# Transposes in place of float32 matmuls, and a new order around q and v, in a hybrid decoder layer

## The chip, the cores and the metric

The kernel runs on one core of a Trainium2 chip, as one launch. The metric is the device time of that launch in microseconds; the median of several runs counts. TensorE is called PE here, VectorE DVE, ScalarE ACT, GpSimd POOL and SyncE SP, as in the profile.

## The reference

One decoder layer on 1024 positions of 1024 features, in float32. A combined input projection feeds two branches, which are gated, merged and added to x; a gated MLP with a short convolution follows.

```python
def rmsnorm(x, gain):
    xf = x.astype(jnp.float32)
    y = xf * lax.rsqrt(jnp.mean(xf * xf, axis=-1, keepdims=True) + NORM_EPS)
    return (y * gain.astype(jnp.float32)).astype(x.dtype)
...
        h = rmsnorm(x, mix_norm[l])
        proj = h @ w_in[l]
        q, k, v, su, sv, g_a, g_b = jnp.split(proj, splits, axis=-1)
        y_att = sliding_window_attention(q, k, v, q_norm[l], k_norm[l], sinks[l])
        y_sgu = chunked_spatial_gating(su, sv, sgu_norm[l], w_s[l], b_s[l])
        merged = (jax.nn.sigmoid(g_a) * (y_att @ w_oa[l])
                  + jax.nn.sigmoid(g_b) * (y_sgu @ w_ob[l]))
        x = x + merged @ w_out[l]
        x = x + conv_gated_mlp(rmsnorm(x, ffn_norm[l]), w_up[l], conv_w[l], conv_b[l], w_down[l])
```

The attention has 8 query heads and 2 key heads of 64 features, a window of 128 positions, and RMS norms of q and k. The MLP is 2816 wide.

## The kernel before

Activations lie transposed, features on the 128 partitions and positions along the free axis. Nearly all products are split: a float32 operand becomes a high and a low part of a faster type (float32r), and three matmuls (high by high, high by low, low by high) stand for one. The large products of the gates, the output projection and the MLP go through a seven-product scheme on half matrices.

The order on each engine is the order in which the code is written (a manual schedule); each engine works through its queue in order and waits where a semaphore says so. So a line that moves in the code moves on its engine's queue, and everything behind it waits with it.

Four places matter.

**The prelude** (lines 427 to 473). k and v have been projected into two PSUM tiles (`pkv`, one for each half of the positions, k and v beside each other). `ss8` holds the sums of x's squares per position, filled by `tsquare`. `k_ms`, `k_norm`, `k_trans`, `k_hi`, `k_lo` and `k_twice` scale k, transpose it and write its high and low parts into `kT`. `v_evac` scales v by `rstd` and takes it out of `pkv` into `vt`. `rstd` is one vector operation and one power on POOL over all eight columns (lines 444 and 451). Between these stand the first four blocks of q: `q_proj` (PE), `q_sq`, `q_ms`, `q_norm` (the scaled block `qr`), `q_trans` (PE, tile `pqt`) and `q_split` (tile `qs`). Half-bank PSUM tiles (`PH`) rotate through four buffers: the matmuls into a tile wait until the readers of the tile four allocations earlier are done. The tiles of the scores (`sc`) take the two buffers that `pkv` had.

**The attention loop** (lines 698 to 745), 20 turns `n`. In turn `n`, PE computes the scores of block `n`, a first filler of other work, the transposes of block `n-2`'s probabilities (`p_trans`, tile `pt`), in eight of the turns from 2 to 13 a second filler (`u_chunk`, twelve 512-column matmuls into `pu`), and then `q_trans(n + 2)`. `q_split(n + 2)` on ACT and DVE follows. In turn 0 `rms_rows` makes `rstd_b`, the eight scale columns as one row over all 1024 positions, repeated on all partitions: a matmul of a repeated column by the identity, in eight pieces (tile `rb`).

**The sum of squares for the second norm** (`ssq_cols`, line 1747, called in `first_pair`, line 1829). `sq2` holds squares summed over the feature tiles; a float32 matmul by a column of ones sums over partitions, in eight pieces of 128 positions. DVE copies the eight columns out, scales them, POOL raises them to -0.5.

**The second broadcast** (`rms`, line 1886, called in `fast_pair` at line 1918) runs `rms_rows` on that result, behind the first product of the next pair. The squares' sum and this broadcast use the same PSUM tile `pb`, the two banks of the next pair's `zv`.

Of the kernel before, what the change touches and what calls it, by code (L numbers as in the profile page):

```python
# [10 lines left out]
F = mybir.dt.float32  # L11
# [3 lines left out]
ALU = mybir.AluOpType  # L15
AX = mybir.AxisListType

S = 1024
D = 1024
# [21 lines left out]
def body(ctx, tc, nc, a):  # L41
# [72 lines left out]
    sink_b = base.tile([128, 8], F, name="sink_b")  # L114
    ident = base.tile([128, 128], F, name="ident")
    rstd_b = base.tile([128, 1024], F, name="rstd_b")
    ones = base.tile([128, 2], F, name="ones")
    mh05 = base.tile([128, 8], F, name="mh05")
    rstd = base.tile([128, 8], F, name="rstd")
    nc.gpsimd.memset(rstd_b[:, 0:128], 1.0)  # L120
    nc.gpsimd.memset(ones, 1.0)
    nc.gpsimd.memset(mh05, -0.5)
    g2 = cp[:, 0:8]
    ng2 = sink_b
# [10 lines left out]
    def rms_rows(pb, col, hs=(0, 1)):  # L135

        for h, p in zip(hs, pb):
            for s in range(4):
                c = 4 * h + s
                nc.tensor.matmul(p[:, s * 128:(s + 1) * 128], col[:, c:c + 1].to_broadcast([128, 128]), ident,  # L140
                                 start=True, stop=True)
        for h, p in zip(hs, pb):
            nc.scalar.copy(rstd_b[:, h * 512:(h + 1) * 512], p)  # L143

# [93 lines left out]
    def tsquare(t):  # L238
        v = xt[t // 4][:, t % 4, :]
        if t in (5, 7):  # L240
            nc.vector.tensor_tensor_reduce(out=v, in0=v, in1=v, scale=1.0, scalar=0.0, op0=ALU.mult, op1=ALU.add,
                                           accum_out=ss8[:, t:t + 1])
            return
        nc.scalar.activation(v, v, AF.Square, accum_out=ss8[:, t:t + 1])
# [130 lines left out]
    def k_ms(h):  # L375
        ss = slice(4 * h, 4 * h + 4)
        nc.vector.tensor_scalar(eps_x[:, ss], ss8[:, ss], EPS / D, EPS * EPS, op0=ALU.mult, op1=ALU.add)
        nc.vector.scalar_tensor_tensor(krs3[:, ss], kss3[:, ss], 1.0 / 64,
                                       eps_x[:, ss].unsqueeze(2).to_broadcast([128, 4, 2]),
                                       op0=ALU.mult, op1=ALU.add)  # L380
        nc.gpsimd.tensor_tensor(krs[:, 8 * h:8 * h + 8], krs[:, 8 * h:8 * h + 8], mh05, op=ALU.pow)
# [32 lines left out]
    def v_evac(h):  # L414
        ss = slice(4 * h, 4 * h + 4)
        nc.vector.tensor_tensor(vt[:, ss, :], pk4[h][:, :, 128:256],
                                rstd[:, ss].unsqueeze(2).to_broadcast([128, 4, 128]), op=ALU.mult)

    def v_split():

        for g in range(2):
            vg_ = vt[:, :, 64 * g:64 * g + 64]
            vh_, vl_ = vhl[:, :, g, 64 * g:64 * g + 64], vhl[:, :, g, 64 - 64 * g:128 - 64 * g]
            copy_hi(vh_, vg_)
            nc.vector.tensor_tensor(vl_, vg_, vh_.bitcast(F), op=ALU.subtract)
# [2 lines left out]
    k_sq(0)  # L428
    k_sq(1)
    k_ms(0)  # L430
    tsquare(4)
    tsquare(5)
    q_proj(0)
# [3 lines left out]
    tsquare(6)  # L437
    q_proj(1)
    tsquare(7)
    q_norm(0)  # L440
    q_sq(1)
    q_ms(1)
    k_ms(1)
    nc.vector.tensor_scalar(rstd, ss8, 1.0 / D, EPS, op0=ALU.mult, op1=ALU.add)
    k_trans(0)
    k_hi(0)
    q_proj(2)
    k_lo(0, (0,))
    q_norm(1)
    k_lo(0, (1,))  # L450
    nc.gpsimd.tensor_tensor(rstd, rstd, mh05, op=ALU.pow)
    k_twice(0)
    q_trans(0)
    q_proj(3)
    q_sq(2)
    q_ms(2)
    k_norm(1)
    q_split(0)
    copy_hi(u_next[0], u_raw[0])
    nc.gpsimd.tensor_tensor(u_next[1], u_raw[0], u_next[0].bitcast(F), op=ALU.subtract)  # L460
    v_evac(0)
    q_norm(2)
    q_trans(1)
    k_trans(1)
# [233 lines left out]
    for n in range(20):  # L698
        if 4 <= n < 12:
            pv_mm(n - 4)  # L700
        if n < 16:
            s_mm(n)
            s_mask(n)
        if 0 <= n - 1 < 16:
            s_exp(n - 1)
        if n < 16:
            s_max(n)
        if 12 <= n:
            pv_mm(n - 4)
        q_new = filler(n, 0)  # L710
        if n == 0:
            for h in (0, 1):
                rms_rows([PH("rb")], rstd, (h,))
        if 0 <= n - 2 < 16:
            p_trans(n - 2)
        filler(n, 1)
        if 0 <= n - 4 < 16:
            pv_out(n - 4)
        for q in q_new:
            q_sq(q)  # L720
            q_ms(q)
        if 0 <= n - 2 < 16:
            p_split(n - 2)
        weights(n)
        if n in (0, 2, 4, 5):
            wo_copy((n + 1) // 2)
        if n in (7, 9, 11, 13):
            wo_add((n - 7) // 2)
        if n == 15:
            rows_again(0)  # L730
        if n == 17:
            x_gain(0, (0, 1))
        if n == 18:
            x_gain(0, (2, 3))
        if n == 19:
            x_sums((0, 1), True)
            x_sums((2, 3), True)
        for t, p in u_done:
            nc.vector.tensor_tensor(uT[:, t, :], p, rstd_b, op=ALU.mult)
        u_done.clear()  # L740
        if n + 2 < 16:
            q_trans(n + 2)
            q_split(n + 2)
        for q in [3] + q_new if n == 0 else q_new:
            q_norm(q)
# [368 lines left out]
    class Blocks:  # L1114
# [9 lines left out]
            if self.zv is not None:  # L1124
                self.v0, self.v1 = self.zv[:, L], self.zv[:, H]

        def prod(self, o, l, r, more=False):
            (wh, wl), y, nk = self.w[l], self.y[r], self.nk
            for k in range(nk):
                for j, (p, q) in enumerate(((wh, 0), (wh, 1), (wl, 0))):  # L1130
                    m = y[:, q, k, :] if nk == 4 else y[:, 2 * q + k, :]
                    nc.tensor.matmul(o, p[:, k, :], m, start=not more and k == 0 and j == 0,  # L1132
                                     stop=k == nk - 1 and j == 2, skip_group_check=True)
# [612 lines left out]

    def ssq_cols(p):
        for s in range(8):
            nc.tensor.matmul(p[:, 2 * s:2 * s + 2], pools["sq2"][:, s * 128:(s + 1) * 128], ones,
                             start=True, stop=True)  # L1750
        pool = pools["fp"]
        ss = pool.tile([128, 8], F, name="ss8b")
        nc.vector.tensor_copy(ss, p[:, 0:16].rearrange("p (s two) -> p s two", two=2)[:, :, 0])
        rsqrt_cols(ss, ss, 8, D)
        return ss

# [72 lines left out]
    def first_pair():  # L1829
        w, nx = lefts[0], lefts[1]  # L1830
        pools["mr_cm"].__exit__(None, None, None)
        pools["ex"] = ctx.enter_context(tc.tile_pool(name="ex", bufs=1, side="right", reuse_waits="tile"))
        z = PS("pz"), PS("pz")
        q, q2 = Pair(0, w.w, z[::-1]), Pair(1, nx.w)
        xu = pools["fp"].tile([128, 1024], F, tag="xu", name="xu")
        x7, u2 = xu[:, L], xu[:, H]
        x1 = pools["wx"].tile([128, 512], F, tag="x1f", name="x1f")

        q.prod(q.v1, "A11", "B11")
        a22_split()  # L1840
        nc.scalar.copy(x1, q.v1)
        fax_split()
        nx.load_p()
        nx.load_q()
        nx.load_s3()
        q.prod(q.g1, "S1", "T1")
        for e in (0, 1):
            right_split_hi("T2", e, ob["B"][:, 2 * e:2 * e + 2, :])
        for e in (0, 1):
            right_split_lo("T2", e, ob["B"][:, 2 * e:2 * e + 2, :])  # L1850
        nc.scalar.copy(u2, q.g1)
        lefts[2].load_ahead()
        q.prod(q.v0, "S3", "T3")
        square("21", 0)
        nx.adds()
        square("21", 1)
        nc.scalar.copy(x7, q.v0)
        for e in (0, 1):
            for i in (0, 1):
                d = 2 * e + i  # L1860
                p = ob["X"][e][:, i, :]
                stt(p, p, gain("21", d)[0], ob["B"][:, d, :], ALU.add)
        for e in (0, 1):
            right_split("T4", e, ob["X"][e])
        q.prod(q.g1, "S4", "B22", more=True)
        q.prod(q.g0, "A12", "B21")
        nc.vector.tensor_tensor(q.g0, q.g0, x1, op=ALU.add)
        sub(nc.vector, x7, x7, u2)
        q.prod(q.v1, "S2", "T2", more=True)
        nx.split_p()  # L1870
        q.prod(q.v0, "A22", "T4", more=True)
        pb = q2.zv
        ratio = ssq_cols(pb)
        nx.split_s3()
        nx.sum_s2()
        nx.sum_s4()
        lefts[2].adds()
        nx.split_q_half(0)
        nx.split_q_half(1)
        lefts[2].load_p()  # L1880
        nc.scalar.copy(u2, q.v1)
        q.u2 = u2
        sub(nc.vector, q.v1, x7, u2)
        sub(nc.vector, q.v0, q.v0, u2)

        def rms():

            rms_rows([pb[:, L], pb[:, H]], ratio)
            q.scale(q.zv)
            q.last_sum()  # L1890

        pools["ft_cm"] = tc.tile_pool(name="ft", bufs=1, reuse_waits="tile")
        return q, q2, rms
# [409 lines left out]
```

## Time and profile before

| | |
|---|---|
| median of 3 runs | 1157.84 us (1157.07 to 1158.2) |
| the profiled execution's own time | 1157.13 us |
| its span, first to last instruction | 1155.4 us |
| PE, POOL, DVE, ACT busy, 0 to 165 us (input projection, attention) | 163.6, 104.9, 119.4, 107.2 us |
| the same, 165 to 535 us (gating unit, gates, merge, output projection) | 369.8, 257.9, 254.1, 213.9 us |
| the same, 535 to 547 us (sum of squares, second broadcast) | 12.0, 9.7, 6.7, 4.8 us |
| the same, 547 to 1115 us (MLP) | 568.0, 285.8, 456.1, 253.5 us |
| the same, 1115 to 1155.4 us (last products, stores) | 37.0, 0, 20.7, 9.2 us |

A row of the timeline reads: start in us, duration in us, engine, line, operation, tile written and tiles read, sizes, count; in brackets the idle time before it and what ended it. Matmuls are pipelined: each is shown with its full duration, and the next one starts before it ends, so what a matmul costs PE is the distance between starts. PEld is the weight load ahead of a matmul. A row of a group (by line or by tile) has the count, the busy time and the mean duration in ns. A row of the view of waits has who waited for whom, the time in us in total, how often, and the longest.

### The profile page before, as it was taken

The page shows a single profiled execution, that of the slowest core. Times are in us where ns is not written, and L with a number is a line of the kernel's source. Part 1 is how long each engine was busy: PE and PEld are TensorE (multiplying, and loading weights), DVE is VectorE, ACT ScalarE, POOL GpSimd, SP SyncE. Part 2 cuts the span into 40 slices and gives each one's busy share as a digit, 9 for nine tenths or more (in the row PEclk, how much of TensorE's full clock was granted, in tenths as well). Part 3 has the DMA queues.
Part 4 walks back from the last instruction along what each step waited for, and adds up shares of the span by engine and source line. Part 5 has one row for each costly group of instructions (what it writes and reads, how often), then busy time and mean ns, then how long its engine had stood idle before and what let it go on. Part 6 is the DMA issues. An engine that isn't in the chain of part 4 may idle for free.

```text
span 1155.4 us, 15810 instructions
## 1 busy us (share of the span) xinstructions
PE 1150.4 (100%) x5789; PEld 978.1 (85%) x5789; DVE 857.0 (74%) x987; ACT 588.7 (51%) x896; POOL 658.3 (57%) x461
## 2 busy tenths in 40 slices
PE   9999999999999999999999999999999999999998
PEld 9999999888888888888888888888888888888887
DVE  7787747734436889887998978797788887766664
ACT  6665568643436546686444444444444354425231
POOL 1768674598783755798877676767676730000000
PEclk9999999999999999999999999999999999999999
DMA  9443565265747766644655554645464358966571
GB/s 367 149 147 67 137 217 201 74 209 174 202 108 240 240 213 237 191 143 120 165 166 149 152 137 137 173 129 145 131 171 134 111 201 308 353 220 197 176 229 56
DMA packets 86429, 204.37 MB, mean 177 GB/s; under 512 B 9616, under 2 KB 17296, under 8 KB 86160
## 3 DMA queue, kind: packets, MB, share of 16 engines
q1 hardware_dynamic: 77280, 174.93, 43.9%
q0 software_dynamic: 8544, 19.93, 10.4%
q10 hardware_dynamic: 528, 8.52, 2.1%
q8 instruction: 45, 0.74, 0.3%
q14 instruction: 32, 0.26, 0.1%
HBM read 162.70 MB, written 57.41 MB: 191 GB/s over the span
## 4 chain that ended last, share of the span: by engine, by line
PE 93%; POOL 3%; DMA 2%; DVE 1%; issue 1%; SPq 0%; ACT 0%; POOLq 0%
PE pz L1132 56%; PE pdx L2083 9%; PE pd L2083 8%; PE pY L1723 2%; PE pX L1723 2%; POOL wjl L1591 1%; PE pu L94 1%; PE pu L92 1%; PE pu L93 1%; PE pvs L94 1%; PE pvs L92 1%; PE pvs L93 1%; PE pv L568 1%; PE pq L92 1%; PE pq L93 1%; PE pq L94 1%
## 5 line engine op out<-in xcount | busy, mean ns | idle before, releaser
L1132 PE MATMUL pz<-T,qh 128*128 128x512 f32 x464 | 143.0, 389 | 0.0
L1132 PE MATMUL pz<-B,ph 128*128 128x512 f32 x352 | 108.6, 390 | 0.0
L1132 PEld LDWEIGHTS pz<-T,qh 128*128 128x128 f32 x464 | 87.0, 188 | 18.3 <-ACT u L949 0.3
L1084 POOL TENSOR_TENSOR pl<-lp,ph 128x1024 fp32r<-128x1024 f32 x30 | 73.3, 2443 | 37.0 <-ACT ph L88 37.0
L1132 PE MATMUL pz<-T,ql 128*128 128x512 f32 x232 | 90.3, 389 | 0.0
L1150 DVE TENSOR_TENSOR pz<-pz,rstd_b 128x1024 f32<-128x1024 f32 x60 | 73.9, 1232 | 6.1 <-ACT rstd_b L143 4.1
L1132 PEld LDWEIGHTS pz<-B,ph 128*128 128x128 f32 x352 | 65.9, 188 | 13.6
L1084 POOL TENSOR_TENSOR ql<-lq,qh 128x1024 fp32r<-128x1024 f32 (+1 forms) x31 | 76.4, 2488 | 0.0
L1132 PE MATMUL pz<-T,s3h 128*128 128x512 f32 x232 | 71.4, 389 | 0.0
L1132 PE MATMUL pz<-y,wjh 128*128 128x512 f32 x224 | 69.5, 391 | 0.1
L1132 PE MATMUL pz<-B,pl 128*128 128x512 f32 x176 | 68.6, 390 | 0.1
L88 ACT ACTIVATE qh<-lq 128x1024 fp32r<-128x1024 f32 (+1 forms) x31 | 31.5, 1020 | 69.3 <-POOL pl L1084 47.4
L1084 POOL TENSOR_TENSOR s3l<-lq,s3h 128x512 fp32r<-128x512 f32 x20 | 26.0, 1301 | 65.9 <-ACT s3h L88 65.9
L1372 POOL TENSOR_TENSOR wjl<-wj,wjh 128x512 fp32r<-128x512 f32 (+1 forms) x32 | 42.0, 1332 | 35.6 <-ACT wjh L88 29.8
L1132 PE MATMUL pz<-B,AX 128*128 128x512 f32 x252 | 60.6, 389 | 0.0
L1132 PE MATMUL pz<-T,AX 128*128 128x512 f32 x252 | 60.5, 389 | 0.0
L2083 PE MATMUL pdx<-bh,ah 128*128 128x512 f32 x152 | 59.2, 390 | 0.0
L2083 PE MATMUL pdx<-bh,al 128*128 128x512 f32 x152 | 59.1, 389 | 0.0
L2083 PE MATMUL pdx<-bl,ah 128*128 128x512 f32 x152 | 59.1, 389 | 0.0
L1144 ACT COPY u<-pz 128x512 f32<-128x512 f32 x28 | 16.4, 587 | 80.8 <-DVE pz L1143 80.8
L1771 DVE SCALAR_TENSOR_TENSOR tg<-pz,cp,tg 128x1023 f32<-128x1023 f32 (+1 forms) x44 | 56.2, 1278 | 0.8
L1771 DVE SCALAR_TENSOR_TENSOR tv<-pz,cp,tv 128x1023 f32<-128x1023 f32 (+1 forms) x44 | 56.2, 1278 | 0.8
(402 smaller groups left out, 3574.6 us busy)
## 6 DMA issues: line engine op xcount, KB each, us to landing
lp<-wup SPq DMA_DIRECT2D x22, 512.0 KB, 3.8
lq<-wup SPq DMA_DIRECT2D x22, 512.0 KB, 4.1
ra<-wdown SPq DMA_DIRECT2D x44, 256.0 KB, 4.5
b<-T SPq DMA_DIRECT2D x44, 256.0 KB, 3.7
lq<-wup POOLq DMA_DIRECT2D x42, 256.0 KB, 5.1
B<-tv SPq DMA_DIRECT2D x33, 256.0 KB, 2.3
T<-tt SPq DMA_DIRECT2D x33, 256.0 KB, 2.1
b<-B SPq DMA_DIRECT2D x33, 256.0 KB, 3.0
```

Source lines behind the costliest of these rows:

```text
L88: return nc.scalar.activation(dst, src, AF.Copy, scale=scale)
L92: nc.tensor.matmul(out, wh, mh, start=first, stop=False, **kw)
L93: nc.tensor.matmul(out, wh, ml, start=False, stop=False, **kw)
L94: nc.tensor.matmul(out, wl, mh, start=False, stop=last, **kw)
L1084: nc.gpsimd.tensor_tensor(l, r, h.bitcast(F), op=ALU.subtract)
L1132: nc.tensor.matmul(o, p[:, k, :], m, start=not more and k == 0 and j == 0, stop=k == nk - 1 and j == 2, skip_group_check=True)
L1144: nc.scalar.copy(self.u2, self.v1)
L1150: nc.vector.tensor_tensor(z, z, rstd_b, op=ALU.mult)
L1372: nc.gpsimd.tensor_tensor(l[:, k], r[:, k], h[:, k].bitcast(F), op=ALU.subtract)
L1723: nc.tensor.matmul(ob[o][e][:, d, :], p[:, 4 * d + k, :], m[:, q, k, :], start=s in (0, 5) and k == 0 and i == 0, stop=k == 3 and i == 2, ...
L1771: nc.vector.scalar_tensor_tensor(t[:, j:], p[:, 0:1024 - j], cw[:, ci, 2 - j:3 - j], t[:, j:], op0=ALU.mult, op1=ALU.add)
L2083: nc.tensor.matmul(o[d], p[:, k - k0, m], q[:, k - k0, :], start=new and k == 0 and j == 0, stop=k == HK - 1 and j == 2, skip_group_check= ...
```

## The change

Four edits.

1. `rms_rows` uses `nc.tensor.transpose` of the repeated column where it had a matmul of it by the identity. The result is the same.
2. `ssq_cols` transposes each 128x128 piece of `sq2` and lets DVE sum along the free axis, where a matmul by ones summed and DVE copied eight columns. The tile `ones` is gone (a pad keeps the addresses). The call moves: `prod` takes a range of k, the last product of the first pair is cut in two, and the sum stands between the halves; a subtraction on DVE (`x7 - u2`) moves behind it.
3. v's scale is made by halves (`v_ms`, `v_pow`) and each half is put on its queue as early as its input is there; `v_evac(0)` moves ahead of `q_norm(1)`, and both parts of `k_lo(0)` move behind `q_norm(1)`, the second one behind `q_ms(2)`.
4. In the attention's turns from 2 on `q_trans(n + 2)` stands directly behind `p_trans(n - 2)`, ahead of the second filler.

```diff
     rstd_b = base.tile([128, 1024], F, name="rstd_b")
-    ones = base.tile([128, 2], F, name="ones")
+    base.tile([128, 2], F, name="pad_b")
...
-                nc.tensor.matmul(p[:, s * 128:(s + 1) * 128], col[:, c:c + 1].to_broadcast([128, 128]), ident,
-                                 start=True, stop=True)
+                nc.tensor.transpose(p[:, s * 128:(s + 1) * 128], col[:, c:c + 1].to_broadcast([128, 128]), ident)
...
+    def v_ms(h):
+        ss = slice(4 * h, 4 * h + 4)
+        nc.vector.tensor_scalar(rstd[:, ss], ss8[:, ss], 1.0 / D, EPS, op0=ALU.mult, op1=ALU.add)
+
+    def v_pow(h):
+        ss = slice(4 * h, 4 * h + 4)
+        nc.gpsimd.tensor_tensor(rstd[:, ss], rstd[:, ss], mh05[:, :4], op=ALU.pow)
...
     k_ms(0)
+    v_ms(0)
     tsquare(4)
...
     tsquare(7)
+    v_pow(0)
     q_norm(0)
     q_sq(1)
     q_ms(1)
     k_ms(1)
-    nc.vector.tensor_scalar(rstd, ss8, 1.0 / D, EPS, op0=ALU.mult, op1=ALU.add)
+    v_ms(1)
     k_trans(0)
     k_hi(0)
     q_proj(2)
+    v_evac(0)
+    q_norm(1)
     k_lo(0, (0,))
-    q_norm(1)
-    k_lo(0, (1,))
-    nc.gpsimd.tensor_tensor(rstd, rstd, mh05, op=ALU.pow)
+    v_pow(1)
     k_twice(0)
     q_trans(0)
     q_proj(3)
     q_sq(2)
     q_ms(2)
+    k_lo(0, (1,))
     k_norm(1)
     q_split(0)
     copy_hi(u_next[0], u_raw[0])
     nc.gpsimd.tensor_tensor(u_next[1], u_raw[0], u_next[0].bitcast(F), op=ALU.subtract)
-    v_evac(0)
     q_norm(2)
...
             p_trans(n - 2)
+        if 2 <= n and n + 2 < 16:
+            q_trans(n + 2)
         filler(n, 1)
...
         if n + 2 < 16:
-            q_trans(n + 2)
+            if n < 2:
+                q_trans(n + 2)
             q_split(n + 2)
...
-        def prod(self, o, l, r, more=False):
+        def prod(self, o, l, r, more=False, ks=None):
             (wh, wl), y, nk = self.w[l], self.y[r], self.nk
-            for k in range(nk):
+            for k in ks or range(nk):
...
-            nc.tensor.matmul(p[:, 2 * s:2 * s + 2], pools["sq2"][:, s * 128:(s + 1) * 128], ones,
-                             start=True, stop=True)
+            c = slice(s * 128, (s + 1) * 128)
+            nc.tensor.transpose(p[:, c], pools["sq2"][:, c], ident)
         pool = pools["fp"]
         ss = pool.tile([128, 8], F, name="ss8b")
-        nc.vector.tensor_copy(ss, p[:, 0:16].rearrange("p (s two) -> p s two", two=2)[:, :, 0])
+        nc.vector.tensor_reduce(ss, p.rearrange("p (s d) -> p s d", d=128), axis=AX.X, op=ALU.add)
...
         nc.vector.tensor_tensor(q.g0, q.g0, x1, op=ALU.add)
-        sub(nc.vector, x7, x7, u2)
         q.prod(q.v1, "S2", "T2", more=True)
         nx.split_p()
-        q.prod(q.v0, "A22", "T4", more=True)
+        q.prod(q.v0, "A22", "T4", more=True, ks=(0, 1))
         pb = q2.zv
         ratio = ssq_cols(pb)
+        sub(nc.vector, x7, x7, u2)
+        q.prod(q.v0, "A22", "T4", more=True, ks=(2, 3))
```

DVE's queue in the prelude, before, from the scale of v on (`rstd`; `kT` is k's low part, `qr` a scaled block of q, `kr` the scaled k, `qs` a split block of q, `vt` the evacuated v):

```order
L444 TENSOR_SCALAR rstd<-ss_124 128x8
L406 SCALAR_TENSOR_TENSOR kT_107<-pk_511,kgq,kT_107 64x512
L339 TENSOR_TENSOR qr_544<-pq_473,qss_503 128x256
L406 SCALAR_TENSOR_TENSOR kT_107<-pk_511,kgq,kT_107 64x512
L331 TENSOR_REDUCE qss_580<-qsq_578 128x4
L332 TENSOR_SCALAR qss_580<-qss_580,eps_x 128x4
L385 TENSOR_TENSOR kr<-pkv_126,krs 128x512
L354 TENSOR_TENSOR qs_585<-pqt_550,qs_585 64x256 x2
L416 TENSOR_TENSOR vt<-pkv_125,rstd 128x512
```

The same place of DVE's queue in the changed kernel:

```order
L419 TENSOR_SCALAR rstd<-ss_123 128x4
L414 TENSOR_TENSOR vt<-pkv_124,rstd 128x512
L337 TENSOR_TENSOR qr_545<-pq_473,qss_504 128x256
L404 SCALAR_TENSOR_TENSOR kT_106<-pk_512,kgq,kT_106 64x512
L329 TENSOR_REDUCE qss_581<-qsq_579 128x4
L330 TENSOR_SCALAR qss_581<-qss_581,eps_x 128x4
L404 SCALAR_TENSOR_TENSOR kT_106<-pk_512,kgq,kT_106 64x512
L383 TENSOR_TENSOR kr<-pkv_125,krs 128x512
L352 TENSOR_TENSOR qs_587<-pqt_551,qs_587 64x256 x2
```

`vt` went from behind `qs` to the front; the first `kT` went behind `qr`, the second behind the two rows of `qss`.

PE's queue in turn 2 of the attention, before, at the end of the second filler (`pu`), q's transposes (`pqt`) and the next scores (`sc`):

```order
L92 MATMUL pu_695<-x_6_119,u0h 128x512
L93 MATMUL pu_695<-x_6_119,u0h 128x512
L94 MATMUL pu_695<-x_6_119,u0l 128x512
L345 MATMUL pqt_891<-ident,qr_732 128x128 x2
L493 MATMUL sc_901<-kT_107,qs_806 128x256 x2
```

The same turn in the changed kernel, at the beginning of that filler:

```order
L546 MATMUL pt_860<-ident,c_651 128x128 x4
L343 MATMUL pqt_865<-ident,qr_733 128x128 x2
L92 MATMUL pu_696<-x_5_117,u0h 128x512
L93 MATMUL pu_696<-x_5_117,u0h 128x512
L94 MATMUL pu_696<-x_5_117,u0l 128x512
```

The two transposes of q moved from behind the twelve matmuls of the filler to the front of them, right behind the four of the probabilities.

PE's queue around the squares' sum, before (`T` with `qh` and `ql`: the last product of the first pair; `B` with `ph`: the first one of the next):

```order
L1132 MATMUL pz_5436<-T_702_5514,ql_5455 128x512
L1132 MATMUL pz_5436<-T_702_5514,qh_5454 128x512 x2
L1132 MATMUL pz_5436<-T_702_5514,ql_5455 128x512
L1749 MATMUL pz_5439<-ones,sq_4748 128x2 x8
L1132 MATMUL pz_5438<-B_659_5112,ph_5557 128x512 x2
```

The same place in the changed kernel:

```order
L1143 MATMUL pz_5437<-T_702_5515,ql_5456 128x512
L1761 MATMUL pz_5440<-ident,sq_4749 128x128 x8
L1143 MATMUL pz_5437<-T_702_5515,qh_5455 128x512 x2
L1143 MATMUL pz_5437<-T_702_5515,ql_5456 128x512
L1143 MATMUL pz_5437<-T_702_5515,qh_5455 128x512 x2
L1143 MATMUL pz_5437<-T_702_5515,ql_5456 128x512
L1143 MATMUL pz_5439<-B_659_5113,ph_5557 128x512 x2
```

The eight instructions became transposes (read: the identity and `sq`) and moved ahead of the product's last six matmuls.

1 line of the change is left out of this document (removed).

## The prediction

> **What bounds the kernel now.** The page comes first: the span, the busy share of each engine, and the clock that TensorE was granted.
>
> ```profile
> span 1155.4 us, 15810 instructions
> PE 1150.4 (100%) x5789; PEld 978.1 (85%) x5789; DVE 857.0 (74%) x987; ACT 588.7 (51%) x896; POOL 658.3 (57%) x461
> PEclk9999999999999999999999999999999999999999
> ```
>
> TensorE is busy for the whole span at full clock; no other engine is busy for over 74%. So time can be won in two ways only: less work on PE, or a shorter wait of PE where one is left. For the second, the view of waits is asked for the weight loads, since a load stands ahead of each matmul and shows a wait that the modelled ends of the matmuls hide.
>
> ```profile
> PEld pz L1132 <- POOL pl L1084: 0.5, 1, 0.5
> PEld pq L92 <- PE pqt L345: 0.4, 1, 0.4
> PEld sc L493 <- issue: 0.3, 1, 0.3
> 547.00:1115.00 568.00, 568.00 (x2507) 470.27 (x2507) 456.14 (x435) 253.53 (x291) 285.78 (x167) 1.00 0.58 177
> ```
>
> The first three rows are among the longest waits of the program: half a microsecond each. The fourth, from the view by stretches, is the MLP: 568.00 us, all of them busy on PE. Whatever PE saves ahead of 547 us is not waited for afterwards and should reach the end.
>
> **The three broadcast and sum steps.** Two edits turn float32 matmuls into transposes: the scale's broadcast (run once at 43.7 us and once at 543 us) and the squares' sum at 538 us, eight instructions each. What they cost is read from starts on the timeline, not from durations, since matmuls overlap.
>
> ```profile
> 43.74 1.95 PE L140 MATMUL rb<-ident,rstd 128*128 128x128 f32 x16
> 45.76 0.39 PE L93 MATMUL pu<-x,u0h 128*128 128x512 f32 x1
> 538.41 1.84 PE L1749 MATMUL pz<-ones,sq 128*128 128x2 f32 x16
> 540.67 0.40 PE L1132 MATMUL pz<-B,pl 128*128 128x512 f32 x1
> 540.90 0.62 PE L1132 MATMUL pz<-B,ph 128*128 128x512 f32 x2
> 58.92 0.60 PE L538 MATMUL pt<-ident,c 128*128 128x128 f32 x4
> 59.58 0.40 PE L93 MATMUL pu<-x,u0h 128*128 128x512 f32 x1
> L345 PE MATMUL pqt<-ident,qr x32: 271/272/273, 35.5 to 137.8; 128*128 128x128 f32 x32
> L140 PE MATMUL pz<-ident,ss8b x16: 271/275/275, 543.0 to 544.6; 128*128 128x128 f32 x16
> ```
>
> One 512-column matmul takes 540.90 - 540.67 = 0.23 us of PE. From 43.74 to 45.76 stand the eight broadcasts and one such matmul: 2.02 - 0.23 = 1.79 us. From 538.41 to 540.67 stand the eight sums and two: 2.26 - 0.46 = 1.80 us. Both show 16 records for eight instructions, so a float32 matmul runs twice, at 0.112 us each, whether it has 128 columns or 2. The transposes of the attention show one record each (32 records for 16 blocks of two). Four of them take 59.58 - 58.92 - 0.23 = 0.43 us, 0.109 each, and eight will take **0.87 us**.
>
> The saving is 1.79 - 0.87 = 0.92 at each broadcast (the second one's row has the same count and duration) and 0.93 at the sum: **2.77 us**. No row shows a transpose whose stationary operand is one column repeated. Its cost lies between 0.87 us for eight (the column costs nothing, as in the matmuls: the repeated column at 43.74 and the plain squares at 538.41 both take 1.8) and the present 1.79. I take 0.87, from the nearer rows.
>
> The Trainium skill, on the page "TensorE: Matmul & The Clock Gate", section "Part 4: PE-mode transpose", gives about 275 ns for one 128x128 transpose inside a kernel, and says that transposes do not bring the clock to its full rate. This trace agrees on the duration (272 ns) and not on the price, since the starts are 0.109 us apart, nor on the clock, which the profile's row shows at 90% or more in every slice, those of the attention's transposes among them. Taken as a price, the page's figure would make eight cost 2.2 us and this edit a loss; that case is a rival below.
>
> **The new chain of the squares' sum.** The sums now stand six matmuls sooner, at 538.41 - 6 x 0.23 = 537.05 us (all in the times of this trace). Behind them VectorE sums 1024 elements where it copied 8, then come POOL's power and the broadcast.
>
> ```profile
> L331 DVE TENSOR_REDUCE qss<-qsq 128x4 f32<-128x256 f32 x16 | 6.7, 417 | 0.8 <-ACT qsq L326 0.2
> L520 DVE TENSOR_REDUCE sm<-c 128x4 f32<-128x516 f32 x16 | 11.0, 689 | 1.5 <-POOL c L510 1.5
> 536.35 2.76 DVE L672 TENSOR_TENSOR xu<-xu 128x512 f32<-128x512 f32 x1
> 536.15 2.40 POOL L1084 TENSOR_TENSOR pl<-lp,ph 128x1024 fp32r<-128x1024 f32 x1
> 540.74 2.05 POOL L131 TENSOR_TENSOR ss8b<-ss8b,mh 128x8 f32<-128x8 f32 x1 [2.18 <-DVE ss8b L130]
> ```
>
> A reduction takes 0.417 us for 256 elements and 0.689 for 516, so about 1.2 for 1024 (an estimate from these two). The transposes end at 537.05 + 0.87 + 0.2 for the last one's run = 538.1; the reduction at 539.3; the small scale op about 0.2 later; POOL's power, 2.05 us, at 541.7. PE comes to the broadcast at 542.97 - 0.93 = 542.05, so the chain is hidden with 0.2 us to spare, if the reduction starts at once. The subtraction at 536.35 took 2.76 us beside POOL's pl and ended right behind it, at 539.1. That is why the change puts it behind the reduction. Were the reduction held up in the same way, until 538.55, PE would wait some 0.2 us. I take 0.05, which also covers the copy of x1 that PE waits for behind the shorter broadcast. The Trainium skill ("SBUF - State Buffer", section "Who interferes with whom") says that a VectorE op with two SBUF inputs and a POOL op that reads SBUF exclude each other, and that a reduction never contends. By this rule the reduction starts at once; if it held for every VectorE op, the sum would be 0.2 us worse.
>
> **v's scale and evacuation.** This moves a wait rather than work. PE's waits ahead of the attention hang on VectorE's queue:
>
> ```profile
> 36.10 0.36 PE L92 MATMUL pq<-wq,x 128*128 128x256 f32 x1 [0.23 <-DVE qr L339]
> 39.20 0.63 PE L392 MATMUL pk<-ident,kr 128*128 128x128 f32 x4
> 39.92 0.47 PE L493 MATMUL sc<-kT,qs 128*128 128x256 f32 x2
> 34.48 0.16 DVE L444 TENSOR_SCALAR rstd<-ss 128x8 f32<-128x8 f32 x1
> 35.55 0.41 DVE L339 TENSOR_TENSOR qr<-pq,qss 128x256 f32<-128x256 f32 x1
> 35.98 0.76 DVE L406 SCALAR_TENSOR_TENSOR kT<-pk,kgq,kT 64x512 fp32r<-64x512 f32 x1
> 37.49 0.69 DVE L385 TENSOR_TENSOR kr<-pkv,krs 128x512 f32<-128x512 f32 x1
> 38.19 0.86 DVE L354 TENSOR_TENSOR qs<-pqt,qs 64x256 fp32r<-64x256 f32 x2
> 39.08 0.69 DVE L416 TENSOR_TENSOR vt<-pkv,rstd 128x512 f32<-128x512 f32 x1
> 34.35 1.01 POOL L333 TENSOR_TENSOR qss<-qss,mh 128x4 f32<-128x4 f32 x1 [1.89 <-DVE eps_x L377]
> ```
>
> Now: q_proj(3) starts 0.15 us behind qr (a buffer); k_trans(1) starts 0.15 us behind qs (38.19 + 0.86 = 39.05; a buffer again); the first scores start 0.15 us behind vt (39.77), whose PSUM tile they take. The change moves vt from 39.08 to right behind rstd. There it takes 0.69 us, from 34.65 to 35.35, while VectorE would wait for POOL's qss, done at 35.36, in any case. So qr comes at 35.4 instead of 35.55, and q_proj(3) gains 0.15. But the first kT, which stood ahead of qr, now stands behind it with its 0.76: 35.85 to 36.6. The second kT, the reduction and the small op take as long as now, 37.49 - 35.98 = 1.5 us, which gives 38.1. kr then ends at 38.75, qs at 39.6 instead of 39.05, and k_trans(1) starts at 39.75 instead of 39.20. The scores no longer wait for vt and follow after four transposes, 0.47 us: 40.2 instead of 39.92. **A loss of 0.3 us.** At best it is nothing (the small op and the kT overlap better), at worst the full 0.55 by which qs is late.
>
> **q's transposes behind the probabilities'.** Eight of the twelve moved pairs change their place; the other four have no work between the two spots.
>
> ```profile
> 66.00 0.60 PE L538 MATMUL pt<-ident,c 128*128 128x128 f32 x4
> 66.89 0.40 PE L568 MATMUL pv<-cl,vhl 128*128 128x256 f32 x2
> 82.64 0.42 DVE L339 TENSOR_TENSOR qr<-pq,qss 128x256 f32<-128x256 f32 x1
> 84.08 0.60 PE L538 MATMUL pt<-ident,c 128*128 128x128 f32 x4
> 87.26 0.38 PE L345 MATMUL pqt<-ident,qr 128*128 128x128 f32 x2
> ACT qs L88 <- PE pqt L345: 16.9, 9, 2.4
> DVE qs L354 <- ACT qs L88: 16.0, 10, 2.5
> ```
>
> At 66.00 the six already stand together: 0.89 us with two 256-column matmuls (0.23), so 0.66, or 6 x 0.11. A run of four costs the same per transpose, so nothing is saved by joining them: 0, or at most 0.1 us in all. ScalarE and VectorE can split q some 2.8 us (twelve matmuls) sooner, in time in which they wait now (16.9 and 16.0 us in the last two rows); PE does not wait for them here. The moved instruction needs qr. In the tightest block qr ends at 83.06 and the new place is 84.08 + 0.44 = 84.52: 1.46 us are left.
>
> **Sum.** -2.77 + 0.05 + 0.3 = -2.4 us against the profiled execution's own 1157.13 (span 1155.4 and 1.7 around it): 1154.7. The median of the runs is 0.7 above that execution, so **1155.4 us**, 0.21% faster. A measurement of this kernel tells about 0.2% (2.3 us) from no change, so the forecast lies on that line.
>
> **Rivals.** *Part of the saving is lost to POOL between 487 and 520 us.* There POOL runs almost without a break.
>
> ```profile
> 486.38 1.06 ACT L88 ACTIVATE wjh<-ow 128x1024 fp32r<-128x1024 f32 x1 [2.48 <-PE pY L1723]
> 487.52 3.77 POOL L1591 TENSOR_TENSOR wjl<-ow,wjh 128x512 fp32r<-128x512 f32 x2 [1.85 <-ACT wjh L88]
> ```
>
> PE's wait for pl (0.5 us, above) ends this stretch. If POOL did not follow PE's earlier arrival, the 0.92 - 0.3 won before it would be gone and 1.8 left: 1156.0. Against it: the stretch begins with a wait for ScalarE, which waits for PE, so it shifts with PE.
>
> *The transposes cost what their duration says.* 8 x 0.272 = 2.18 us against 1.79, three times: +1.2, and +0.3: 1159.3. Starts 0.109 us apart in runs of four and six speak against it. If instead the compiler ran each twice, as now, nothing would be saved: 1158.1.
>
> *Slower: PE stands still in front of q's transposes.* They now block twelve 512-column matmuls (12 x 0.23 = 2.8 us) that had covered a late qr. From 1.46 us of lateness in the tightest block each further microsecond is PE's; once it passes 0.3 us a block over eight blocks, the 2.4 us are gone. If qr came only when the transposes stand today, 8 x 2.8 = 22 us would be lost: 1177. Against it: the same move lets VectorE start earlier, since q's split is what it waits for.
>
> *More is won:* the prelude loses nothing and joins save 0.1: 1155.0.
>
> **How the numbers follow.** Forecast 0.60 (its own range 1154.9 to 1155.9, a little over half of it below the line at 1155.5); more won 0.12; part lost 0.18; transposes dearer 0.05; PE behind qr 0.05. Faster 0.47, within 0.2% 0.48, slower 0.05. The range, 1154.3 to 1157.0, takes in the first three, the bounds of the prelude and of the reduction, and the spread of the runs; it leaves out the last two.
>
> **What would show it.** Eight records instead of 16 at each of the three places, 0.11 us apart; the reduction near 1.2 us, with PE reaching the second broadcast without a wait; k_trans(1) later behind qs and the scores right behind it; no wait of PE for qr in the attention; the stretch from 547 us on as long as before. The forecast is wrong if transposes of a repeated column start 0.2 us apart or if a wait on POOL near 520 us grows by what was won ahead of it.

## The result, and the profile after

The changed kernel takes **1156.15 us** (median of 20 runs, 1155.07 to 1157.84), the kernel before 1157.74 in runs beside it. The ratio is 0.9986, with an interval of [0.998, 0.9992]: 0.14% faster. The profiled execution has a span of 1153.5 us, 1.9 less than before; the forecast for it was 2.4 less. Between the medians lie 1.59 us.

The page first: span, busy engines and the granted clock.

```profile
span 1153.5 us, 15760 instructions
PE 1148.4 (100%) x5765; PEld 976.6 (85%) x5765; DVE 855.6 (74%) x988; ACT 588.4 (51%) x896; POOL 659.5 (57%) x461
PEclk9999999999999999999999999999999999999999
```

PE has 24 records fewer, eight for each of the three steps, and still bounds the kernel. Next the view of waits, for the weight loads (engine and line, what it waited for, us in total, times, the longest).

```profile
PEld pk L390 <- PE pqt L343: 0.7, 1, 0.7
...
PEld pz L1143 <- POOL pl L1095: 0.5, 1, 0.5
...
PEld pz L1143 <- DVE x L680: 0.4, 1, 0.4
```

POOL's pl is waited for as before. Two rows are new among the longest: the late k_trans(1), which was forecast (put down here to the last transposes ahead of it; its row on the timeline, below, names qs), and a wait for VectorE's x, which was not.

The timeline shows the three steps themselves.

```profile
43.95 1.03 PE L139 MATMUL rb<-ident,rstd 128*128 128x128 f32 x8
44.74 0.48 PE L92 MATMUL pu<-x,u0h 128*128 128x512 f32 x1
45.05 0.40 PE L93 MATMUL pu<-x,u0h 128*128 128x512 f32 x1
...
535.76 2.39 POOL L1095 TENSOR_TENSOR pl<-lp,ph 128x1024 fp32r<-128x1024 f32 x1
...
536.71 1.03 PE L1761 MATMUL pz<-ident,sq 128*128 128x128 f32 x8
...
537.50 0.71 PE L1143 MATMUL pz<-T,qh 128*128 128x512 f32 x2
537.78 1.22 DVE L1764 TENSOR_REDUCE ss8b<-pz 128x8 f32<-128x1024 f32 x1 [1.74 <-PE pz L1761]
...
538.04 0.39 PE L1143 MATMUL pz<-T,ql 128*128 128x512 f32 x1
...
539.12 0.69 DVE L680 TENSOR_TENSOR xu<-xu 128x512 f32<-128x512 f32 x1
...
539.28 2.05 POOL L130 TENSOR_TENSOR ss8b<-ss8b,mh 128x8 f32<-128x8 f32 x1 [1.13 <-DVE ss8b L129]
...
541.67 1.04 PE L139 MATMUL pz<-ident,ss8b 128*128 128x128 f32 x8
...
542.51 0.72 PE L1143 MATMUL pz<-B,ph 128*128 128x512 f32 x2
```

From 43.95 to 45.05 stand eight transposes and one 512-column matmul: 1.10 - 0.23 = 0.87 us, as forecast; the squares' transposes and two such matmuls take 538.04 - 536.71 = 1.33, again 0.87 for the eight. The reduction takes 1.22 us, POOL's power ends at 541.33, and PE reaches the second broadcast at 541.67 without a wait.

**Where the 1.9 us come from.** Each matmul is set beside the same one of the kernel before (same tiles, same count), and the median difference of their starts is taken in several stretches. The table gives what each stretch adds (us; below zero is sooner). The first column holds how late PE is ahead of the first broadcast; it differs from execution to execution. The kernels of the experiments stand in it too, but for extra_pair, which adds work.

| kernel | up to 43 us | first broadcast | attention, 46 to 140 | 140 to 532 | sum and second broadcast, to 547 | 547 to 610 | at the end |
|---|---|---|---|---|---|---|---|
| forecast | +0.3 | -0.92 | 0 | 0 | -1.80 | 0 | -2.42 |
| changed kernel | +0.21 | -0.91 | +0.43 | -0.08 | -1.81 | +0.23 | -1.91 |
| changed_again | +0.71 | -0.91 | +0.30 | -0.11 | -1.81 | +0.59 | -1.21 |
| two_moved | +0.69 | -0.93 | +0.33 | -0.14 | -1.81 | +0.37 | -1.51 |
| no_q_move | +0.14 | -0.91 | +0.15 | -0.15 | -1.81 | +0.31 | -2.26 |
| no_v | +0.39 | -0.93 | +0.41 | +0.45 | -1.81 | -0.01 | -1.50 |
| three_transposes | +0.64 | -0.91 | +0.15 | -0.12 | -1.81 | +0.03 | -2.02 |
| three_again | +1.38 | -0.93 | +0.13 | -0.02 | -1.81 | +0.55 | -0.69 |
| sum_early | +0.09 | -0.93 | +0.05 | +0.02 | -1.79 | +0.46 | -2.11 |
| sum_early_again | +0.44 | -0.91 | +0.15 | -0.20 | -1.79 | -0.01 | -2.33 |
| sum_only | +0.93 | -0.03 | +0.02 | -0.21 | -0.95 | -0.06 | -0.30 |
| broadcasts_only | +0.52 | -0.91 | +0.15 | -0.09 | -0.85 | +0.96 | -0.22 |
| q_only | +0.39 | -0.03 | +0.30 | +0.07 | 0 | -0.06 | +0.67 |

The three steps give what was forecast, in every kernel that has them. The half microsecond that is missing in the changed kernel was lost in the attention and behind 547 us, where nothing was forecast. That the first column comes near its forecast is chance: v's part costs 0.05 us of the 0.21 (below), and the other 0.16 is a later start of VectorE's first kr (31.67 us against 31.51).

### The profile page after: what moved, and what is told of

It is laid out like the page before. It is cut to its first block, busy times and chain, and to the rows that moved or that the text cites. A ratio compares the mean times of both kernels' runs of the same rounds, so it can differ in the third digit from the quotient of the medians.

```text
span 1153.5 us, 15760 instructions
## 1 busy us (share of the span) xinstructions
PE 1148.4 (100%) x5765; PEld 976.6 (85%) x5765; DVE 855.6 (74%) x988; ACT 588.4 (51%) x896; POOL 659.5 (57%) x461
## 4 chain that ended last, share of the span: by engine, by line
PE 99%; DVE 1%; issue 0%; POOL 0%; POOLq 0%
PE pz L1143 56%; PE pdx L2095 9%; PE pd L2095 8%; PE pX L1734 4%; PE pY L1734 3%; PE pkv L279 2%; PE pu L94 1%; PE pu L92 1%; PE pu L93 1%; PE pvs L93 1%; PE pvs L92 1%; PE pvs L94 1%; PE pv L576 1%; PE pq L94 1%; PE pq L93 1%; PE pq L92 1%
```

## The experiments

### The place of q's transposes

**two_moved**: the transposes moved in two blocks only.

```diff
-        if 2 <= n and n + 2 < 16:
+        if n in (6, 10):
             q_trans(n + 2)
...
-            if n < 2:
+            if n not in (6, 10):
                 q_trans(n + 2)
```

> The changed kernel, but q's transposes stand behind the probabilities' in two of the twelve blocks only (n = 6 and n = 10); in the other ten they stand where they stood before. Theory (pace): where the move takes the two transposes away from the place ahead of pv, the 24 projections of the next block run 0.118 us apart instead of 0.1133, 0.1 us a block. Then the projections that follow block 6 and block 10 (near 89 and 118 us) take 2.83 us from their first start to the next transpose, and those near 75, 97 and 110 us take 2.74 us. Rival (chance or a shift): the pace of the changed kernel's attention has to do with its earlier start or with that execution, not with the place of the transposes; then all five blocks stay at 2.83 us, or others than those two are slow.

Measured: one run, 1155.62 us, span 1153.9. The timeline of PE shows the first projection of a block and the transposes that follow its 24.

```profile
89.14 0.28 PE L92 MATMUL pq<-wq,x 128*128 128x256 f32 x1
91.97 0.60 PE L546 MATMUL pt<-ident,c 128*128 128x128 f32 x4
97.27 0.28 PE L92 MATMUL pq<-wq,x 128*128 128x256 f32 x1
100.00 0.60 PE L546 MATMUL pt<-ident,c 128*128 128x128 f32 x4
110.73 0.28 PE L92 MATMUL pq<-wq,x 128*128 128x256 f32 x1
113.47 0.60 PE L546 MATMUL pt<-ident,c 128*128 128x128 f32 x4
```

Behind block 6 the 24 projections take 91.97 - 89.14 = 2.83 us; in the blocks that were not moved 2.73 and 2.74. The one behind block 10 takes 2.83, the one near 76 us 2.74. So the pace goes with the move, block by block. But the projections near 102 us are now slow too (2.83), which neither the kernel before nor the changed one has, and no theory foretold that.

**no_q_move**: the changed kernel with all transposes at their old place (both edits of the loop undone).

> The changed kernel with q's transposes at their old place in all blocks; the broadcasts, the squares' sum and v's part stay as changed. Theory (pace): all five blocks near 75, 89, 97, 110 and 118 us are back at 2.74 us, the offset against the kernel before stays near -0.7 us from 45 to 160 us, and the span is 0.4 us shorter than the changed kernel's 1153.5: near 1153.1, a ratio of 0.998 to the kernel before. Rival (the move costs nothing): the attention loses the same 0.4 us, span 1153.5, ratio 0.9986.

Measured: 1155.48 us, ratio 0.9981 [0.9972, 0.999], span 1153.2. The same place on its timeline, ahead of that of the changed kernel:

```profile
88.63 0.28 PE L92 MATMUL pq<-wq,x 128*128 128x256 f32 x1
...
91.36 0.38 PE L546 MATMUL pt<-ident,c 128*128 128x128 f32 x2
```

```profile
88.78 0.28 PE L92 MATMUL pq<-wq,x 128*128 128x256 f32 x1
...
91.61 0.27 PE L546 MATMUL pt<-ident,c 128*128 128x128 f32 x1
```

2.73 us against 2.83. In the kernel before, the same block took 92.10 - 89.36 = 2.74:

```profile
89.36 0.28 PE L92 MATMUL pq<-wq,x 128*128 128x256 f32 x1
...
92.10 0.60 PE L538 MATMUL pt<-ident,c 128*128 128x128 f32 x4
```

All five blocks are back at 2.73 or 2.74, and the attention loses 0.15 instead of 0.43 us; of the 0.15, 0.09 lie in the block near 102 us. The span is 0.3 us shorter, not the 0.4 that was expected, and times this close are not told apart by their intervals.

**q_only**: the kernel before with this move alone.

> The kernel before with q's transposes behind the probabilities' and nothing else. Theory (pace): the projections of the five blocks near 75, 89, 97, 110 and 118 us take 2.83 us instead of 2.74, PE is 0.4 us later at 160 us than it was relative to it at 60 us, and the kernel is 0.3 to 0.4 us slower than before: ratio 1.0003. Rival (it costs nothing, the prediction's): ratio 1.0000, offset the same at 60 and at 160 us.

Measured: 1158.34 us, ratio 1.0005 [0.9996, 1.0014]; by time alone not told from no change. On the trace the five blocks take 2.83 us, and the attention loses 0.30 us. The move does cost what the theory says, though part of it is given back, since the block near 49 us is faster here (2.73 instead of 2.83).

**extra_pair**: the changed kernel with two transposes more ahead of pv in two blocks.

```diff
             if n < 2:
                 q_trans(n + 2)
+            if n in (6, 10):
+                pd = PH("pd")
+                for t in range(2):
+                    nc.tensor.transpose(pd[:, t * 128:(t + 1) * 128], ident, ident)
```

> The changed kernel with two transposes more at the old place (of the identity, into a PSUM tile of their own that nobody reads), in blocks 6 and 10 only; q's own transposes stay behind the probabilities'. Theory (what stands ahead of pv): a pair of transposes between the 512-column matmuls and pv sets the pace of the projections behind, whatever it transposes. Then the projections near 89 and 118 us take 2.74 us, those near 75, 97 and 110 us stay at 2.83, and the two pairs add 4 x 0.11 = 0.44 us on PE and give back 0.2. Rival (the place behind the probabilities'): the six transposes that stand together set the pace; then 89 and 118 stay at 2.83 us.

Measured: one run, 1159.62 us, span 1157.9. It loses far more than its two pairs, since the two tiles shift the ring of PSUM buffers: near 200 us PE waits 1.7 us for VectorE. Only the pace is read from it, again on PE's timeline.

```profile
87.37 0.38 PE L757 MATMUL pd<-ident 128*128 128x128 f32 x2
87.90 0.47 PE L576 MATMUL pv<-eh,vhl 128*128 128x256 f32 x2
...
89.86 0.28 PE L92 MATMUL pq<-wq,x 128*128 128x256 f32 x1
...
92.60 0.60 PE L546 MATMUL pt<-ident,c 128*128 128x128 f32 x4
```

The projections from 89.86 to 92.60 take 2.74 us, as do those near 120 us; the three blocks without a pair stay at 2.83. So in these blocks it is the pair ahead of pv, whatever it transposes, and not the six transposes that stand together. Why a pair there should set the pace is not shown.

### v's scale and evacuation

**no_v**: the changed kernel with `v_ms`, `v_pow`, `v_evac(0)` and `k_lo` back in the order of before.

> The changed kernel with v's scale, its first evacuation and k_lo where they were before. Theory (the prediction's): v's part costs 0.28 us, because k_trans(1) starts behind a later qs; undone, k_trans(1) starts near 39.2 us and the first scores some 0.28 us sooner than the changed kernel's 40.13, span near 1153.2. Rival (it costs nothing): the later k_trans(1) is made good since the scores no longer wait for vt; counted from VectorE's first kr, the scores come 8.4 to 8.5 us later as in both kernels (31.51 to 39.92 before, 31.67 to 40.13 after), span 1153.5 within 0.2.

Measured: 1156.41 us, ratio 0.9989 [0.998, 0.9998]. VectorE and PE in the prelude, first of the changed kernel, then of no_v:

```profile
31.67 0.69 DVE L383 TENSOR_TENSOR kr<-pkv,krs 128x512 f32<-128x512 f32 x1 [0.55 <-POOL krs L379]
...
34.72 0.68 DVE L414 TENSOR_TENSOR vt<-pkv,rstd 128x512 f32<-128x512 f32 x1
...
38.74 0.86 DVE L352 TENSOR_TENSOR qs<-pqt,qs 64x256 fp32r<-64x256 f32 x2
...
39.74 0.63 PE L390 MATMUL pk<-ident,kr 128*128 128x128 f32 x4 [0.49 <-DVE qs L352]
40.13 0.48 PE L501 MATMUL sc<-kT,qs 128*128 128x256 f32 x2
```

```profile
31.94 0.69 DVE L383 TENSOR_TENSOR kr<-pkv,krs 128x512 f32<-128x512 f32 x1 [0.97 <-POOL krs L379]
...
38.63 0.86 DVE L352 TENSOR_TENSOR qs<-pqt,qs 64x256 fp32r<-64x256 f32 x2
39.52 0.69 DVE L414 TENSOR_TENSOR vt<-pkv,rstd 128x512 f32<-128x512 f32 x1
...
39.63 0.63 PE L390 MATMUL pk<-ident,kr 128*128 128x128 f32 x4
40.35 0.47 PE L491 MATMUL sc<-kT,qs 128*128 128x256 f32 x2
```

From the first kr to k_trans(1) are 8.07 us with the change and 7.69 without; to the first scores 8.46 and 8.41. Over all executions the scores come 8.45 to 8.46 us behind kr with v's part (five executions) and 8.40 to 8.42 without (nine, the kernel before among them). k_trans(1) is 0.38 us late, and the wait of the scores for vt, gone, gives 0.33 back: **v's part costs 0.05 us.** The one piece of it ahead of kr, `v_ms(0)` (0.16 us on VectorE), costs nothing there, since kr waits 0.55 us for POOL in any case. The longer span of no_v's profiled execution (1153.9) has another cause: near 205 us PE waits 0.6 us for ScalarE, which had itself waited 1.1 us for a load of x near 179 us; VectorE carries 0.57 us of this lateness to 205 us. three_transposes has no such wait.

### The wait behind 547 us

**three_transposes**: the broadcasts and the sum alone, without v's part and without the move.

> Only the two broadcasts and the squares' sum by transposes, with the sum's place and the moved subtraction; q's transposes and v's part as before. Theory (pace and v's cost both): 0.92 + 0.92 + 0.93 less 0.05 for the sum's chain and 0.2 for the wait near 594 us: 2.5 us off the kernel before, span near 1152.9, ratio 0.9978. Theory (pace alone): the same 1152.9 to 1153.2, as v's part is worth nothing. Rival (neither costs anything): span 1153.5, ratio 0.9986.

Measured: 1155.53 us, ratio 0.9978 [0.9969, 0.9987], span 1153.4. The stretch behind 547 us loses 0.03 us where the changed kernel lost 0.23, with the same instructions there.

**sum_only** and **broadcasts_only** do one part each.

> Only the squares' sum by transposes (with its place and the moved subtraction); both broadcasts stay float32 matmuls. Theory: PE is 0.88 us sooner behind the second broadcast than before and POOL's power 1.1 us sooner, so POOL is ahead of PE and there is no new wait near 594 us; 0.9 us off the kernel before, ratio 0.9992. Rival (the sum's chain costs PE time at the second broadcast): PE waits ahead of the broadcast and the gain is under 0.6 us.

> Only the two broadcasts by transposes; the squares' sum stays a float32 matmul at its old place. Each broadcast gives 0.92 us on PE. Theory (POOL's lag): POOL's power moves only with the first, so behind the second POOL is 0.92 us behind PE, more than the 0.65 us of the changed kernel, and PE waits near 594 us for VectorE's x by 0.3 to 0.6 us: 1.3 to 1.5 us off the kernel before at the end, ratio 0.9988. Rival (chance of the load): no wait there, 1.84 us, ratio 0.9984.

Measured: sum_only 1157.31 us, ratio 0.9994 [0.9985, 1.0003]; PE is 0.95 us sooner behind the second broadcast and loses nothing later. broadcasts_only 1157.1 us, ratio 0.9998 [0.9989, 1.0007]: of 0.91 + 0.85 us won, 0.96 are lost again behind 547 us, more than either theory gave. Its ScalarE, and its weight loads:

```profile
553.60 0.63 ACT L88 ACTIVATE s3h<-lq 128x512 fp32r<-128x512 f32 x1 [3.51 <-DMA lq<-wup]
```

```profile
576.84 2.14 PEld L1131 LDWEIGHTS pz<-B,AX 128*128 128x128 f32 x10 [0.74 <-DVE x L671]
```

ScalarE's s3h waits for a load of the MLP's weights that POOL's queue issues; what follows on ScalarE, POOL and VectorE up to x hangs on it, and PE waits for x.

**sum_early**: three_transposes with the sum 0.68 us sooner.

```diff
-        q.prod(q.v0, "A22", "T4", more=True, ks=(0, 1))
+        q.prod(q.v0, "A22", "T4", more=True, ks=(0,))
         pb = q2.zv
         ratio = ssq_cols(pb)
         sub(nc.vector, x7, x7, u2)
-        q.prod(q.v0, "A22", "T4", more=True, ks=(2, 3))
+        q.prod(q.v0, "A22", "T4", more=True, ks=(1, 2, 3))
```

> The three transposes alone (v's part and q's transposes as before), with the squares' sum three 512-column matmuls (0.68 us) sooner than in the changed kernel. Theory (POOL's lag): in the changed kernel the power starts 1.45 us sooner than before, PE behind the second broadcast 2.10 us sooner; POOL's queue (the power, the subtractions, the weights' loads behind it) is so 0.65 us behind PE, and PE waits for VectorE's x near 594 us. With the sum 0.68 us sooner POOL moves as far as PE, no new wait near 594 us is left in any execution, and the span is that of three_transposes less what it lost there (0 to 0.2 us): near 1153.0 to 1153.4 with prelude as there. Rival (chance of the load): the wait depends on when a load of weights lands and not on POOL's lag; then POOL's shift of 0.68 us is seen, but not in x, and the span is as in three_transposes. Rival (too early): PE reaches the transposes before the squares are ready (POOL, 535.8 us) and waits up to 0.3 us.

Measured: 1155.16 us, ratio 0.998 [0.9972, 0.9989]. POOL's power starts 2.56 us sooner than before, as far as PE (2.57). Yet 0.46 us are lost behind 547 us, so the main theory fell as it stands: a power that keeps up with PE does not do away with the loss. But POOL's issue of the load of weights (546.57 us before) comes only 2.06 us sooner, since a subtraction on POOL between the power and the issue takes 1.73 us where it took 1.26 before. The three kernels were run once more, together.

> The changed kernel once more. Theory: the pace is a matter of the program, so the projections near 75, 89, 97, 110 and 118 us are at 2.83 us again, and those near 56, 62, 81 us at 2.74; the first scores come 8.46 us behind VectorE's first kr; the wait near 594 us is what x is late against PE (measured from the offsets at 547 us), less 0.1. Rival: these differ from execution to execution as the start does (first kr between 31.5 and 32.5 us so far). Ratio 0.9986 as before.

> The three transposes alone with the sum 0.68 us sooner, once more, beside the changed kernel on the same chip. Theory: 0.4 us faster than the changed kernel for the pace of the projections and as good as equal in the rest: ratio 0.998 to the kernel before, 1155.2 to 1155.6 us. The loss near 594 us follows when the load of weights lands (ScalarE's s3h) and not POOL's power; if this execution's landing is late against PE by another amount than in the last one (0.56 us), the loss differs by as much. Rival: the same loss of 0.46 us again, as a property of the program.

> The three transposes alone, with the sum at the changed kernel's place, once more, beside the two others. Theory: ratio 0.998, as sum_early, since neither the sum's place nor v's part is worth what can be measured; projections near 75, 89, 97, 110 and 118 us at 2.74 us. Rival: the changed kernel and this one are the same to 0.1 us.

Measured: changed_again 1156.36 us, ratio 0.9985 [0.9977, 0.9994]; sum_early_again 1155.04, 0.9976 [0.9967, 0.9986]; three_again 1156.28, 0.9988 [0.9979, 0.9997]. The five blocks have the pace that was expected of each. The losses behind 547 us do not: 0.59, none and 0.55 us, against 0.23, 0.46 and 0.03 in the first executions of the same kernels. ScalarE's s3h, VectorE's x and PE's weight load in the changed kernel, and then in sum_early_again:

```profile
552.01 0.63 ACT L88 ACTIVATE s3h<-lq 128x512 fp32r<-128x512 f32 x1 [3.04 <-DMA lq<-wup]
...
593.75 0.68 DVE L680 TENSOR_TENSOR x<-x,pz 128x512 f32<-128x512 f32 x1
...
594.48 2.59 PEld L1143 LDWEIGHTS pz<-B,AX 128*128 128x128 f32 x12 [0.37 <-DVE x L680]
```

```profile
551.65 0.63 ACT L88 ACTIVATE s3h<-lq 128x512 fp32r<-128x512 f32 x1 [2.94 <-DMA lq<-wup]
...
593.36 0.68 DVE L670 TENSOR_TENSOR x<-x,pz 128x512 f32<-128x512 f32 x1
...
594.09 2.58 PEld L1130 LDWEIGHTS pz<-B,AX 128*128 128x128 f32 x12 [0.19 <-DVE x L670]
```

From s3h to x are 41.74 and 41.71 us: the chain follows the load. In the kernel before it takes 42.67. There POOL waits with its second issue for another load of weights, and VectorE's tt, beside the POOL work that follows, takes 0.95 us longer; up to tt's start it is 5.05 us in the one and 5.06 in the changed kernel. Rows of the kernel before, and then the two of them that differ in the changed one:

```profile
552.89 0.63 ACT L88 ACTIVATE s3h<-lq 128x512 fp32r<-128x512 f32 x1 [1.87 <-DMA lq<-wup]
...
556.72 0.86 POOL L1043 DMA_DIRECT2D lq<-wup  x1 [0.60 <-DMA lq<-wup]
...
557.94 3.87 DVE L672 TENSOR_TENSOR tt<-tv 128x512 f32<-128x512 f32 x1
...
595.56 0.68 DVE L672 TENSOR_TENSOR x<-x,pz 128x512 f32<-128x512 f32 x1
...
596.29 0.84 PEld L1132 LDWEIGHTS pz<-B,AX 128*128 128x128 f32 x4
```

```profile
554.55 1.21 POOL L1054 DMA_DIRECT2D lq<-wup  x1
...
557.07 2.92 DVE L680 TENSOR_TENSOR tt<-tv 128x512 f32<-128x512 f32 x1
```

So the load behind s3h had about 1 us to spare there, though x itself came just in time. Against the kernel before (load issued at 546.57, s3h at 552.89, x at 595.56), with PE's offset at 547 us:

| kernel | PE at 547 us | load issued | s3h | x | x behind PE | lost behind 547 us |
|---|---|---|---|---|---|---|
| no_v | -1.49 | -0.75 | -0.54 | -1.47 | 0.02 | -0.01 |
| sum_early_again | -2.31 | -1.81 | -1.24 | -2.21 | 0.10 | -0.01 |
| three_transposes | -2.05 | -1.31 | -0.93 | -1.91 | 0.14 | 0.03 |
| changed kernel | -2.15 | -1.42 | -0.87 | -1.82 | 0.33 | 0.23 |
| sum_early | -2.57 | -2.06 | -1.06 | -2.00 | 0.57 | 0.46 |
| three_again | -1.25 | -0.51 | +0.33 | -0.63 | 0.62 | 0.55 |
| changed_again | -1.81 | -1.07 | -0.15 | -1.12 | 0.69 | 0.59 |
| broadcasts_only | -1.18 | -0.30 | +0.71 | -0.11 | 1.07 | 0.96 |

What is lost is what x is behind PE, less about 0.1, in each row but the first, where nothing is lost. Two things make s3h late against PE, and they add up. POOL issues the load 0.50 to 0.88 us late against PE (0.73 in the changed kernel, 0.51 in sum_early); this is POOL's lag, and it goes with the program. And s3h starts 6.5 to 7.3 us behind the issue in these executions, 6.3 before: 0.2 to 1.0 us more, which differs between executions of one program. Their sum less 1.05 us, the 0.95 by which the chain is shorter and the 0.1, gives the loss of each row that has one to 0.05 us; in broadcasts_only it gives 0.84 of 0.96, and there the second issue waits as well. Why the load takes longer, and how it could be held to one value, is left open.

## Why the prediction was right or wrong

**The size was nearly right**: 2.4 us forecast on the profiled execution, 1.9 measured; 1155.4 forecast, 1156.15 measured, within the range and short of the 0.2% line. But it lies outside the forecast's own range (1154.9 to 1155.9), and of the medians' difference 1.59 us came of some 2.4. Of the 0.75 us between forecast and median, 0.5 are in the span; the rest is that the median stands 0.93 above the profiled execution, where 0.7 was taken from before. Point by point:

- *The three steps*, 2.77 us less 0.05: right. A transpose with a repeated column costs 0.109 us, as the nearer rows said. The table has -0.91 for the first broadcast and -1.81 for the two others together, forecast -0.92 and -1.80. So the duration of 272 ns, and the rival built on it, does not hold as a price.
- *The new chain of the squares' sum*: right. The reduction took 1.22 us against 1.2, began while POOL's pl still ran (until 538.15) and was not held up. The subtraction that took 2.76 us beside pl takes 0.69 behind it. This agrees with the rule of the Trainium skill ("SBUF - State Buffer", section "Who interferes with whom") on reductions beside POOL; the 0.2 us without it did not arise. PE had 0.34 us to spare at the second broadcast (541.67 less 541.33). The prediction wrote 0.2, but its own figures, 542.05 less 541.7, give 0.35, so a reduction held up until 538.55 would have cost 0.1 and not 0.2.
- *v's scale and evacuation*, "a loss of 0.3 us": the mechanism was right and the size was wrong, 0.05. Counted from the first kr, k_trans(1) was forecast at 39.75 - 31.51 = 8.24 us and came at 8.07; the scores at 8.69 and came at 8.46. VectorE needed 0.17 us less for what it does up to qs, and the scores follow k_trans(1) after 0.39 us, not 0.47.
- *q's transposes*, "0, or at most 0.1 us in all": this step failed. The transposes themselves cost the same at both places, and PE does not wait for qr, as argued. Left out was what the pair ahead of pv does to the 24 projections behind it: five blocks lose 0.1 us each. In the whole attention 0.25 us of it are left, the mean of 0.43, 0.30, 0.41 and 0.30 with the move in all blocks against 0.15, 0.15, 0.13, 0.05, 0.15, 0.02 and 0.15 without.
- *"Whatever PE saves ahead of 547 us is not waited for afterwards"*: this failed too, by 0.23 us in the profiled execution and by up to 0.96 elsewhere. That PE was busy for all of 568 us showed that nothing was late then; it did not show by how little. x was ready 0.05 us ahead of PE's weight load in the kernel before (595.56 + 0.68, against 596.29), and the load behind s3h had about 1 us to spare. What PE gains beyond that, and the load does not share, turns into a wait. (The three waits of PE that were read ahead of this sentence are 0.5, 0.4 and 0.3 us, not half a microsecond each.)
- *The rivals*: part of the gain was lost, as the first rival had it, but behind 547 us and not between 487 and 520, where PE keeps what it has. That 1156.15 stands so near this rival's 1156.0 is chance. PE behind qr and dearer transposes did not come.

Of the versions measured, sum_early has the lowest medians, 1155.16 and 1155.04 us, but beside the changed kernel the intervals overlap (0.9976 [0.9967, 0.9986] and 0.9985 [0.9977, 0.9994]), so that it beats it is likely and not shown. Run beside each other, all ten runs of sum_early_again lie below the changed kernel's median of 1156.36; that is one round.

## What to carry to other kernels

A float32 matmul that only broadcasts or sums costs about twice what the transpose of a 128x128 block costs (0.22 against 0.11 us here), and that saving is read reliably from the starts of the neighbouring rows. An engine that is busy for a whole stretch has no waits there, but it can have hardly any slack either: before a gain is carried through, look how long ahead of it the things are ready that it takes, loads above all. And a move that changes what stands in front of short matmuls can change their pace, so the pace behind the move belongs in the sum.

## What was not expected of the hardware

- *Two paces.* The same 24 256-column matmuls run 0.1133 or 0.118 us apart over a whole block (2.74 or 2.83 us), at a granted clock of 1.00 and without a wait. Over a block the pace is steady, and for most blocks it repeats from execution to execution and goes with what stands ahead of pv. For the blocks near 41, 49 and 102 us it also changes where nothing near them was edited: in three_transposes the one near 41 us took 2.83 us and in three_again 2.74. What sets it is not settled.
- *The start.* VectorE's first kr starts between 31.51 and 32.93 us; in sum_early and three_again, whose programs are the same up to there, at 31.63 and 32.93. This alone moves a span by over 1 us, more than any edit here is worth but the transposes.
- *The load of weights* near 546 us reaches ScalarE's s3h 6.3 to 7.3 us behind its issue, and PE inherits 40 us later what is over the 1 us that the load has to spare.
